# Feed-forward products of a decoder layer by one level of Strassen

## The chip, the cores and the metric

One core of a Trainium2 chip runs the whole program. Its engines are TensorE (PE in the profile, with its weight loads as PEld), VectorE (DVE), ScalarE (ACT), GpSimd (POOL) and SyncE (SP), which here only issues DMAs. The metric is device time in microseconds for one execution. The kernel before takes 2062.53 us, the median of 3 runs (2061.35 to 2063.6).

## The reference

One decoder layer is computed for 1024 prompt tokens and 32 sample tokens (8 sequences of 4), 1056 tokens in all, with model width 1024, in float32:

```python
x = x + 0.5 * _swiglu(_rms(x, g1), w1g, w1u, w1d)
z = _rms(x, gm) @ w_in                    # q, k, v, gate B, gate C, h
x = x + concat([att, gate_b * cv]) @ w_out
x = x + 0.5 * _swiglu(_rms(x, g2), w2g, w2u, w2d)
x = x + sigmoid(_rms(x, gp) @ wpg) * (pe @ wpp)

def _swiglu(h, w_gate, w_up, w_down):
    return (silu(h @ w_gate) * (h @ w_up)) @ w_down
```

The attention is over a sliding window of 128 with a sink for each head, and the convolution is causal with width 3. The feed-forward width is 2816, so the gate and up matrices are 1024 x 2816 and the down matrix is 2816 x 1024. There are two feed-forwards, and they hold 132 of the 166 weight units (a unit is 128 x 1024) that the kernel reads in its main stream.

## The kernel before

**Precision.** Each float32 product is made of three products of float32r parts. A weight or an activation w is split into hi (a rounded copy, made by ScalarE) and lo = w - hi (made by VectorE). `mm_group` (L266) then issues, for each block of 128 rows, hi x hi (L268), lo x hi (L269) and hi x lo (L270) into one PSUM bank.

**Layout.** Activations lie with the model dimension on the partitions: `x[c]` holds 8 blocks of 128 rows for the tokens of chunk c. There are three chunks of 384, 384 and 288 tokens.

**Weights.** All weight units form one list in order of use. `pump_dma` (L96) loads them on SP's queue into two raw buffers, `split_one` (L104) splits one unit on ScalarE (L110) and VectorE (L111), and up to five split units are held. `tick` (L130) counts groups of products. It splits a unit if there is room, and runs work that was put off with `after(d, fn)` until d groups later.

**Norm.** `prep` (L230) splits x times the gain, without the token's factor; `square` (L220) and `norm_r` (L243) compute `rb`, the factor 1/sqrt(mean square) for each token, by squares on ScalarE, adds on GpSimd (L228), a product with ones, and `rsqrt_chain` (L198) on VectorE. The factor multiplies what comes out of the products (L305, L309), so products can start before it is known. For the first feed-forward it comes from a token-major copy of x (L398 to L432).

**Feed-forward.** `ffn` (L282) goes through the 22 blocks of the feed-forward width in groups of 3, 3, 4, 4, 4 and 4. For each block, `gate` and `up` multiply a unit by the three chunks; `up` applies silu and leaves the hidden activation, split, in SBUF (`hh`, `hl`). After each group, `down` (L315) multiplies the group's blocks into the 8 output blocks and adds a quarter of that to `x` (L325). In the last group each output block is followed at once by `prep` and `square` for the next norm (L364 to L366).

**Between the feed-forwards** come the input projection, attention and convolution, worked in pieces between product groups, and the output projection. x waits in DRAM meanwhile (`xs_d`, L456), and `mix` takes its place in SBUF. At the end comes the gated embedding (L905 to L974).

**Order.** The order of each engine's instructions is fixed when the program is built, by the order in which the code names them and by when a model of the chip takes them to be ready. On the chip each engine takes its list in order. Five PSUM banks serve the large products and three the small ones.

## Time and profile before

| | |
|---|---|
| median of 3 runs | 2062.53 us |
| profiled execution: span from first to last instruction | 2060.6 us |
| what lies around the span, against the median | 1.9 us |
| TensorE busy | 2050.2 us (99%), 12683 matmuls |
| VectorE busy | 960.3 us (47%) |
| ScalarE busy | 501.5 us (24%) |
| GpSimd busy | 287.2 us (14%) |
| moved by DMA | 118.06 MB, 57 GB/s on average |

The span is one profiled execution; its time outside the span isn't shown, so it is compared with the median of the runs. A row of the grouped view names line, engine, operation, output and inputs, shapes and count, then the busy time of the group and the mean length of one instruction in ns, then the idle time of the engine before them and what ended it. Matmuls are pipelined: the length of one is its latency, and what a stream of them costs is the distance between their starts. A row of the view by windows gives the busy time of each engine in a stretch, the granted TensorE clock (1.00 is full speed), the DMA engines' share and GB/s.

### The profile page before, as it was taken

How to read it: one execution, taken by the hardware profiler on the slowest of the kernel's cores; microseconds unless marked ns; L12 is line 12 of the kernel's file. 1: busy time of each engine (PE TensorE's matmuls, PEld its weight loads, DVE VectorE, ACT ScalarE, POOL GpSimd, SP SyncE). 2: the span in 40 equal slices, each digit the busy share in tenths (PEclk: the TensorE clock that was granted, in tenths of full speed). 3: DMA queues.
4: the chain of work that ended last, by engine and by line, in shares of the span. 5: the costliest groups of instructions: out<-in, count | busy, mean ns of one | idle time of the engine just before them, and what ended most of it. 6: DMA issues, size and time to landing. Idle time of an engine off the chain costs nothing.

```text
span 2060.6 us, 29941 instructions
## 1 busy us (share of the span) xinstructions
PE 2050.2 (99%) x12683; PEld 2007.9 (97%) x12683; DVE 960.3 (47%) x1809; ACT 501.5 (24%) x917; POOL 287.2 (14%) x335
## 2 busy tenths in 40 slices
PE   9999999999999999999999999999999999999999
PEld 9999999999999999988888999999999999999999
DVE  6343433433334366466773764343333343344843
ACT  6121120211211243233442421212112022023410
POOL 3201010110100142022221220101101001012300
PEclk9999999999999999999999999999999999999999
DMA  7211110211111124111131211111111021111121
GB/s 263 76 54 42 52 52 11 83 41 51 43 32 62 42 102 136 35 31 32 31 93 36 70 52 41 49 38 50 40 52 52 21 72 42 31 62 52 59 71 39
DMA packets 37673, 118.06 MB, mean 57 GB/s; under 512 B 7697, under 2 KB 12185, under 8 KB 36644
## 3 DMA queue, kind: packets, MB, share of 16 engines
q1 hardware_dynamic: 35780, 112.05, 16.9%
q0 software_dynamic: 1472, 4.00, 0.7%
q8 instruction: 99, 1.62, 0.3%
q14 instruction: 34, 0.28, 0.0%
q10 hardware_dynamic: 288, 0.10, 0.0%
HBM read 106.26 MB, written 11.58 MB: 57 GB/s over the span
## 4 chain that ended last, share of the span: by engine, by line
PE 97%; DVE 2%; DMA 1%; ACT 0%; issue 0%; POOL 0%; ACTq 0%; DVEq 0%; POOLq 0%
PE ps L269 29%; PE ps L268 29%; PE ps L270 28%; PE ps L790 2%; PE ps L791 2%; PE ps L792 2%; PE ps L630 1%; PE ps L674 1%; PE ps L627 1%; PE ps L665 1%; PE ps L570 0%; DVE xnl L236 0%; DVE xr L325 0%; DVE wlo L111 0%; DVE nt L209 0%; DMA wraw<-in_wpg_dram 0%
## 5 line engine op out<-in xcount | busy, mean ns | idle before, releaser
L268 PE MATMUL ps<-xnh,whi 128*128 128x384 f32 (+1 forms) x2448 | 786.8, 322 | 1.2 <-ACT whi L110 1.2
L269 PE MATMUL ps<-xnh,wlo 128*128 128x384 f32 (+1 forms) x2448 | 786.7, 322 | 0.8 <-DVE wlo L111 0.8
L270 PE MATMUL ps<-xnl,whi 128*128 128x384 f32 (+1 forms) x2448 | 786.2, 321 | 0.0
L269 PEld LDWEIGHTS ps<-xnh,wlo 128*128 128x128 f32 x2448 | 460.0, 188 | 1.3 <-DVE wlo L111 1.1
L268 PEld LDWEIGHTS ps<-xnh,whi 128*128 128x128 f32 x2448 | 459.8, 188 | 1.5 <-ACT whi L110 1.4
L270 PEld LDWEIGHTS ps<-xnl,whi 128*128 128x128 f32 x2448 | 460.1, 188 | 0.2
L269 PE MATMUL ps<-hh,wlo 128*128 128x384 f32 (+1 forms) x1056 | 343.8, 326 | 0.0
L268 PE MATMUL ps<-hh,whi 128*128 128x384 f32 (+1 forms) x1056 | 341.5, 324 | 0.0
L270 PE MATMUL ps<-hl,whi 128*128 128x384 f32 (+1 forms) x1056 | 336.7, 320 | 0.0
L110 ACT CAST whi<-wraw 128x1024 fp32r<-128x1024 f32 x166 | 173.1, 1051 | 615.9 <-PE ps L270 523.0
L309 POOL TENSOR_TENSOR a<-a,rb 128x384 f32<-128x384 f32 x132 | 128.9, 977 | 1235.8 <-DVE a L308 1230.3
L111 DVE TENSOR_TENSOR wlo<-wraw,whi 128x1024 fp32r<-128x1024 f32 x166 | 213.5, 1290 | 106.8 <-ACT whi L110 106.6
L270 PEld LDWEIGHTS ps<-hl,whi 128*128 128x128 f32 x1056 | 198.1, 188 | 0.9 <-DVE hl L312 0.6
L269 PEld LDWEIGHTS ps<-hh,wlo 128*128 128x128 f32 x1056 | 198.1, 188 | 0.5
L268 PEld LDWEIGHTS ps<-hh,whi 128*128 128x128 f32 x1056 | 197.6, 187 | 0.3
L311 ACT CAST hh<-a 128x384 fp32r<-128x384 f32 x132 | 64.3, 487 | 366.9 <-POOL a L309 366.9
L305 DVE TENSOR_TENSOR a<-ps,rb 128x384 f32<-128x384 f32 x132 | 69.1, 524 | 178.3 <-PE ps L270 174.7
L312 DVE TENSOR_TENSOR hl<-a,hh 128x384 fp32r<-128x384 f32 x132 | 68.8, 521 | 152.0 <-ACT hh L311 152.0
L325 DVE SCALAR_TENSOR_TENSOR xr<-ps,xr 128x384 f32<-128x384 f32 (+1 forms) x144 | 75.2, 523 | 132.8 <-PE ps L270 132.6
L325 DVE SCALAR_TENSOR_TENSOR x<-ps,x 128x384 f32<-128x384 f32 (+1 forms) x144 | 75.1, 522 | 133.0 <-PE ps L270 132.9
L308 DVE TENSOR_TENSOR a<-a,ps 128x384 f32<-128x384 f32 x132 | 68.8, 521 | 126.3 <-PE ps L270 125.7
L306 ACT ACTIVATE th<-a 128x384 f32<-128x384 f32 x132 | 65.5, 496 | 225.8 <-DVE a L305 225.7
(190 smaller groups left out, 1828.6 us busy)
## 6 DMA issues: line engine op xcount, KB each, us to landing
wraw<-in_w1gu_dram SPq DMA_DIRECT2D x44, 512.0 KB
wraw<-in_w2gu_dram SPq DMA_DIRECT2D x44, 512.0 KB
wraw<-in_w1d_dram SPq DMA_DIRECT2D x22, 512.0 KB
wraw<-in_w2d_dram SPq DMA_DIRECT2D x22, 512.0 KB
wraw<-in_win_dram SPq DMA_DIRECT2D x18, 512.0 KB
xtok<-in_xtok_dram SPq DMA_DIRECT2D x8, 512.0 KB
wraw<-in_wout_dram SPq DMA_DIRECT2D x8, 512.0 KB
wraw<-in_wpg_dram SPq DMA_DIRECT2D x8, 512.0 KB
```

What stands on the lines that cost most here:

```text
L110: nc.scalar.copy(out=hi, in_=raw)
L111: nc.vector.tensor_tensor(out=lo, in0=raw, in1=hi.bitcast(F32), op=ALU.subtract)
L268: nc.tensor.matmul(ps[:, :W], lhsT=wh, rhs=xh, start=(k == 0), stop=False)
L269: nc.tensor.matmul(ps[:, :W], lhsT=wl, rhs=xh, start=False, stop=False)
L270: nc.tensor.matmul(ps[:, :W], lhsT=wh, rhs=xl, start=False, stop=(k == n - 1))
L305: nc.vector.tensor_tensor(out=a[:, :W], in0=psg[:, :W], in1=rb, op=ALU.mult)
L306: nc.scalar.activation(out=th[:, :W], in_=a[:, :W], func=AF.Tanh, scale=0.5)
L308: nc.vector.tensor_tensor(out=a[:, :W], in0=a[:, :W], in1=ps[:, :W], op=ALU.mult)
L309: nc.gpsimd.tensor_tensor(out=a[:, :W], in0=a[:, :W], in1=rb, op=ALU.mult)
L311: nc.scalar.copy(out=hh[j][:, sl], in_=a[:, :W])
L312: nc.vector.tensor_tensor(out=hl[j][:, sl], in0=a[:, :W], in1=hh[j][:, sl].bitcast(F32), op=ALU.subtract)
L325: nc.vector.scalar_tensor_tensor(out=x[c][:, m], in0=ps[:, :W], scalar=0.25, in1=x[c][:, m], op0=ALU.mult, op1=ALU.add)
```

## The change

Both feed-forwards are written anew; the projections, attention, convolution and embedding keep their products, with their memory pools opened and closed around them.

**Products.** The product of a 256-row pair of weight blocks with the activations is treated as a 2 x 2 matrix product of half-blocks, by a seven-product form of Strassen's method. The tokens are two halves (c) of 528, each of two quarters of 264; the model dimension has two halves of four 128-row blocks. For gate and up, "2 x 2" on the weight side is the two halves of the rows by gate and up; for down it is the two blocks of a pair by output blocks m and m + 4. Each of seven products is a sum of weight blocks times a sum of activation blocks, made of 264-column matmuls, three for each block of rows. Seven weight operands and seven activation operands are split into hi and lo. Products 1, 6, 7 and 4 accumulate in one PSUM bank with readings in between, 5 and 3 in a second, 2 in a third. `segment` interleaves one quad's products with the rest of the one before.

**Phases.** `gate_up` first makes the normalised activations of a token half (`normed`: squares, rb, then for each of 4 block pairs the sums on GpSimd and seven splits), then goes through the 22 blocks j with their two halves. The first two blocks run for the first half, then for the second (their weights are loaded twice), so that the second half's activations are made meanwhile. The hidden activations go to DRAM (`hd`). `down` reads them back in four groups of 2, 3, 3 and 3 pairs (`hidden`), makes their sums and splits, and adds the products to X.

**Norms.** `prep`, `square` and `norm_r` for the input projection and the embedding stand behind `down`, no longer within its last group.

```diff
-    def ffn(tag, name, g_next, name_next, s_next, skew):
...
+    def weights(pr, po, blocks, wd, shape):
+        r = []
+        for b in blocks:
+            t = pr.tile([P, wd], F32, name="wr", tag="wr", bufs=6)
+            nc.sync.dma_start(out=t.rearrange("p (k m) -> p k m", m=P), in_=b)
+            r.append(t)
+        s = [pr.tile([P, wd], F32, name="ws", tag="ws", bufs=4) for _ in range(4)]
+        add = nc.gpsimd.tensor_tensor
+        add(out=s[0], in0=r[2], in1=r[3], op=ALU.add)
+        add(out=s[1], in0=s[0], in1=r[0], op=ALU.add)
+        add(out=s[2], in0=r[0], in1=r[2], op=ALU.add)
+        add(out=s[3], in0=s[1], in1=r[1], op=ALU.add)
+        of = {1: r[0], 2: r[1], 3: s[3], 4: r[3], 5: s[0], 6: s[1], 7: s[2]}
+        for o in OPS:
+            hi = po.tile([P, wd], F32R, name=f"wh{o}", tag=f"wh{o}")
+            lo = po.tile([P, wd], F32R, name=f"wl{o}", tag=f"wl{o}")
+            split(hi, lo, of[o])
...
+        def product(self, o, ps, start):
+            wh, wl = self.w[o]
+            bh, bl = self.acts[o]
+            for k in range(self.n):
+                ks = slice(k * P, (k + 1) * P)
+                last = k == self.n - 1
+                nc.tensor.matmul(ps[:, :HH], lhsT=wh[:, ks], rhs=bh[:, k], start=(start and k == 0), stop=False, skip_group_check=True)
+                nc.tensor.matmul(ps[:, :HH], lhsT=wl[:, ks], rhs=bh[:, k], start=False, stop=False, skip_group_check=True)
+                nc.tensor.matmul(ps[:, :HH], lhsT=wh[:, ks], rhs=bl[:, k], start=False, stop=last, skip_group_check=True)
...
+    def segment(q, p):
+        for o, of in ((1, q), (5, q), (7, p), (2, q), (6, q), (3, p), (4, p)):
+            if of:
+                of.step(o)
...
+    class Down(Quad):
+        def add(self, x, h, ps, f):
+            s = slice(h * HH, (h + 1) * HH)
+            nc.vector.scalar_tensor_tensor(out=x[:, s], in0=ps[:, :HH], scalar=f, in1=x[:, s], op0=ALU.mult, op1=ALU.add)
...
+    def normed(pool, c, g):
...
+        for k in range(4):
+            y = [wtile(f"y{j}", shape=[P, 2, HH]) for j in range(2)]
+            for j in range(2):
+                kk = k + 4 * j
+                nc.vector.scalar_tensor_tensor(
+                    out=y[j].rearrange("p n t -> p (n t)"), in0=X[kk][c], scalar=vec[:, g + kk:g + kk + 1], in1=rb, op0=ALU.mult, op1=ALU.mult,
+                )
+            sums(acts, k, y[0][:, 0], y[0][:, 1], y[1][:, 0], y[1][:, 1], wtile("ta", shape=[P, 2, HH]), wtile("tb", shape=[P, 2, HH]))
+        return acts
+
+    def sums(acts, k, b11, b12, b21, b22, ta, tb):
+        nt3, nt1, nt2, nt4 = ta[:, 0], ta[:, 1], tb[:, 0], tb[:, 1]
+        tt = nc.gpsimd.tensor_tensor
+        tt(out=nt1, in0=b11, in1=b12, op=ALU.subtract)
+        tt(out=nt3, in0=b12, in1=b22, op=ALU.subtract)
+        tt(out=nt2, in0=nt3, in1=b11, op=ALU.subtract)
+        tt(out=nt4, in0=nt2, in1=b21, op=ALU.add)
...
+    def gate_up(gu, g, spill, mid=None):
...
+        plan = [(j, (0,)) for j in range(SKEW)] + [(j, (1,)) for j in range(SKEW)] + [(j, (0, 1)) for j in range(SKEW, FF)]
...
+    def down(dn, src):
...
+        def hidden(gi, c):
+            p0, n = DGROUPS[gi]
+            t = ph[0].tile([P, 2, 2, n, HH], F32, name="hr", tag="hr")
+            for i in range(2):
+                for h in range(2):
+                    o = c * HC + h * HH
+                    nc.sync.dma_start(out=t[:, i, h], in_=hd[2 * p0 + i:2 * (p0 + n) + i - 1:2, :, o:o + HH].rearrange("q p t -> p q t"))
+            a = {}
+            for o in OPS:
+                a[o] = tuple(pa[c][0].tile([P, n, HH], F32R, name=f"h{u}{o}", tag=f"h{u}{o}") for u in "hl")
...
+    gate_up(w1gu, G1, False, bias_table)
+    down(w1d, xin)
...
+    for c in range(3):
         for k in range(KT):
-            prep(c, k, G2)
+            prep(c, k, GP)
             square(c, k)
-        norm_r(c, "n2", 8)
...
+        norm_r(c, "np", 9, 4 if c < 2 else 2)
```

Each pool that `gate_up`, `down` and the middle part open takes SBUF that others have closed; a tile waits for the earlier tiles that lay there. Every tile of these pools has one buffer unless the code names more (6 raw weight tiles, 4 weight sums); each activation and weight operand has one.

551 lines of the change are left out of this document (322 added, 229 removed).

## The prediction

> **What bounds the kernel now.** I read the page's busy shares first, then the chain that ended last, then what TensorE waited for.
>
> ```profile
> PE 2050.2 (99%) x12683; PEld 2007.9 (97%) x12683; DVE 960.3 (47%) x1809; ACT 501.5 (24%) x917; POOL 287.2 (14%) x335
> PE 97%; DVE 2%; DMA 1%; ACT 0%; issue 0%; POOL 0%; ACTq 0%; DVEq 0%; POOLq 0%
> ```
>
> ```profile
> PE ps L268 <- ACT whi L110: 1.2, 1, 1.2
> ```
>
> TensorE is busy 99% of the span and is 97% of the chain; its longest wait is 1.2 us. So a matmul removed is time removed, as long as the other engines stay hidden, and only about 10 us in the whole span are idle to be won. VectorE has half the span free, GpSimd most of it.
>
> A matmul's price is its start-to-start distance, not its "mean ns" (that is latency, and matmuls overlap). A stretch of the timeline inside the first feed-forward gives it for both widths in use:
>
> ```profile
> 299.75 0.29 PE L268 MATMUL ps<-xnh,whi 128*128 128x288 f32 x1
> ...
> 302.15 0.34 PE L268 MATMUL ps<-xnh,whi 128*128 128x384 f32 x1
> ...
> 310.47 0.29 PE L268 MATMUL ps<-xnh,whi 128*128 128x288 f32 x1
> ```
>
> 18 matmuls of 288 columns start in 2.40 us (133.3 ns each), 48 of 384 in 8.32 us (173.3 ns). A line through both: 0.417 ns a column and 13.3 ns for each matmul whatever its width.
>
> **What is removed.** Each feed-forward has (44 gate and up units x 8 + 22 down units x 8) x 3 products x 3 chunks = 4752 matmuls; a triple of chunks takes 2 x 173.3 + 133.3 = 480 ns, so 1584 x 480 = 760 us. The change has 22 x 2 halves x 7 x 12 = 3696 and 11 x 4 x 2 x 7 x 3 = 1848, together 5544 matmuls of 264 columns: more matmuls, though an eighth fewer columns. At 264 columns the line gives 123.3 ns, 684 us. **Saved: 76.7 us each, 153 us for both**, not the 190 us that an eighth of 1520 would be. No row has 264 columns. If 264 columns cost what 288 do (133.3 ns), both save 42 us; if time were proportional to columns (122.2 ns), 166 us. I take the line, whose nearest point is 24 columns away.
>
> **What the other engines are given.** The rows that price it (mean ns is the number before the bar of idle time):
>
> ```profile
> L111 DVE TENSOR_TENSOR wlo<-wraw,whi 128x1024 fp32r<-128x1024 f32 x166 | 213.5, 1290 | 106.8 <-ACT whi L110 106.6
> L312 DVE TENSOR_TENSOR hl<-a,hh 128x384 fp32r<-128x384 f32 x88 | 49.1, 558 | 149.7 <-ACT hh L311 149.7
> L312 DVE TENSOR_TENSOR hl<-a,hh 128x288 fp32r<-128x288 f32 x44 | 19.6, 446 | 2.3 <-ACT hh L311 2.3
> L325 DVE SCALAR_TENSOR_TENSOR x<-ps,x 128x288 f32<-128x288 f32 x48 | 21.8, 455 | 31.5 <-PE ps L270 31.5
> L311 ACT CAST hh<-a 128x384 fp32r<-128x384 f32 x88 | 45.2, 514 | 346.2 <-POOL a L309 346.2
> L311 ACT CAST hh<-a 128x288 fp32r<-128x288 f32 x44 | 19.1, 434 | 20.7 <-POOL a L309 20.7
> L309 POOL TENSOR_TENSOR a<-a,rb 128x384 f32<-128x384 f32 x88 | 91.3, 1038 | 1137.4 <-DVE a L308 1131.9 <-ACT th L306 5.5
> L309 POOL TENSOR_TENSOR a<-a,rb 128x288 f32<-128x288 f32 x44 | 37.6, 854 | 98.3 <-DVE a L308 98.3
> ```
>
> Scaled to the new widths: DVE about 0.42 us at 264 columns, 0.56 at 384, 0.69 at 512, 0.98 at 792, and 0.43 for a 264-column add from PSUM; ACT 0.41 at 264, 0.62 at 512; POOL 0.80 at 264, 1.28 at 512, 1.82 at 792.
>
> In the middle of gate_up this hides. One j has 168 matmuls, 20.7 us; DVE does 7 x 0.69 + 14 x 0.42 = 10.7 us, ACT 7 x 0.62 + 8 x 0.41 = 7.6 us, POOL 4 x 1.28 + 2 x 0.80 = 6.7 us. I cost it at nothing; the cover is the 20.7 us, and even DVE and POOL in strict turns (17.4 us) fit.
>
> They may have to take turns:
>
> ```profile
> L111 DVE TENSOR_TENSOR wlo<-wraw,whi x166: 1208/1226/2071, 7.7 to 1984.6; 128x1024 fp32r<-128x1024 f32 x166
> L228 POOL TENSOR_TENSOR acc<-acc,sq x63: 803/1018/2253, 735.5 to 1941.8; 128x384 f32<-128x384 f32 x42, 128x288 f32<-128x288 f32 x21
> L325 DVE SCALAR_TENSOR_TENSOR x<-ps,x x144: 441/558/558, 84.5 to 780.9; 128x384 f32<-128x384 f32 x96, 128x288 f32<-128x288 f32 x48
> L236 DVE SCALAR_TENSOR_TENSOR xnl<-x,vec,xnh x48: 502/614/1369, 6.3 to 783.9; 128x384 fp32r<-128x384 f32 x32, 128x288 fp32r<-128x288 f32 x16
> ```
>
> (min/median/max ns.) The same DVE subtraction takes 1.23 us or 2.07 us, the same POOL add 1.02 or 2.25: the extra is about one operation of the other engine. The lines that lengthen have both operands in SBUF; the adds from PSUM (L325) never pass 0.56 us. The Trainium skill, "SBUF — State Buffer", section "Who interferes with whom", says that a VectorE instruction with two SBUF inputs and a GpSimd instruction that reads SBUF exclude each other for the whole instruction. By it every length below is the full sum of both engines; the maxima here agree with that direction.
>
> **The head of each feed-forward.** Today TensorE starts on raw x, since the token factor rb is applied behind the product. The new gate_up needs sums of normalised x, so squares, rb, sums and seven splits stand before the first product. For one half of the tokens: DVE 8 x 0.76 (the gain-times-rb step, L236's 614 stretched to 528 columns) + 28 x 0.42 = 17.9 us; POOL 16 x 0.80 = 12.8 us, in a chain of four each. Overlapped: 17.9 us; in turns: 30.7. I take 26, nearer the turns, because all of these DVE operations have both operands in SBUF, like the lines that lengthen. A weight set (7 splits, 4 adds) is 4.8 to 9.9 us, taken as 8.7. The second half has six more adds, 30 us in all.
>
> ```profile
> 0.74 3.51 DMA x<-in_xT_dram
> ...
> 7.73 0.44 PE L268 MATMUL ps<-xnh,whi 128*128 128x384 f32 x1 [1.15 <-ACT whi L110]
> ```
>
> ```profile
> 0.00:10.00 10.00, 6.94 (x31) 6.39 (x32) 3.69 (x9) 5.66 (x8) 1.22 (x7) 1.00 0.84 310
> 1920.00:1940.00 20.00, 20.00 (x138) 19.73 (x138) 18.75 (x42) 11.85 (x23) 9.16 (x10) 1.00 0.00 1
> 1940.00:1960.00 20.00, 17.19 (x92) 15.48 (x91) 18.50 (x42) 6.58 (x9) 2.59 (x2) 1.00 0.57 178
> ```
>
> (Windows: length, busy PE, PEld, DVE, ACT, POOL, then clock, DMA share, GB/s.) First feed-forward: half of x, 2.2 MB at 310 GB/s behind a first landing at 4.3 us, is there at about 10 us; the last square, add, statistics and rb end at about 16 us by my estimate. Then first half 26, its weights 8.7, second half 30, second weights 8.7: the third segment, the first on the second half, can start at 89 us. TensorE has then done 11 products of 12 matmuls, 16.3 us. Today it begins at 7.7 us and runs some 3 us slow: 89 - 16.3 - 7.7 - 3 = **+62 us** (overlapped +38, in turns +76). The skew of two j gives the second half a cover of those 16 us, against 30 and two weight sets. Second feed-forward: the first half of x is final four groups of 24 x 133.3 ns, 12.8 us, before the output projection ends, and some 6 us of squares, statistics and rb follow, so sums start 7 us before that end: -7 + 26 + 8.7 + 30 + 8.7 - 16.3 = **+50 us** (+26 to +64).
>
> **Entry to down.** The activations' trip through DRAM itself hides, since only the last j's store is fresh and the first group reads j 0 to 3. But the first weights wait for gate_up's buffers:
>
> ```profile
> 1944.45 4.48 DMA wraw<-in_wpg_dram
> ```
>
> A wait for a weight load like this one is 4.5 us, and a split behind it 1 us; the second half's sums then meet segments of only 5.2 us. In the first group (pairs, so 256-column weights) DVE has 28 x 0.41 + 56 x 0.43 + 14 x 0.71 = 45.5 us against TensorE's 41.4. Together 15 us, **+30** for both (10 to 50).
>
> **Group changes in down.** A group of three pairs is 62.2 us on TensorE; DVE has 28 x 0.56 + 56 x 0.43 + 14 x 0.98 = 53.5 us, POOL 16 x 1.04 + 8 x 1.82 = 31 us. Over the group it just fits, but the seven activation tiles and the one load buffer `hr` have no second copy: the second half's load is issued only when the first half's last direct split is done, some 0.8 us into the new group, and 1.6 MB at 310 GB/s plus two POOL sums and a split end at about 13.7 us, where product 6 is wanted at 12.2. With what queues on DVE I take 4 us a change, three a feed-forward: **+24** (10 to 72). SP issues in order, so weight loads behind that waiting load are late too; they have a spare set and half.
>
> **Norms behind down.** Today the last down group's products cover prep, square and the rsqrt chains, though DVE is then 18.75 of 20 us busy (row above). The new code starts them when down's memory is free, in the last three products.
>
> ```profile
> L207 DVE SCALAR_TENSOR_TENSOR nt<-rb 128x192 f32<-128x192 f32 x36 | 14.2, 428 | 0.0
> ```
>
> One chunk is 8 x 0.61 on DVE and up to 8 x 1.0 on POOL, 5 to 13 us, then up to 8 for its rsqrt chain (two halves x ten operations like this one), against 8.3 us of k and v products: **+15** before the input projection (4 to 25), **+12** before the embedding (2 to 25), where 2.8 us of TensorE idle exist already (last window). Reading x back before the output projection has five PSUM buffers of 4.2 us as cover: **+3** (0 to 10). Its stores lie beside k and v.
>
> **The clock.**
>
> ```profile
> 10.25:13.65 3.40, 3.40 (x13) 3.40 (x12) 3.00 (x6) 3.40 (x7) 0.00 (x0) 0.52 1.05 420
> ```
>
> After the waits at the start TensorE ran 3.4 us at half clock, 1.7 us lost. Some ten new stops could each bring one: 0 to 17 us, **+8** taken, as most stops end in work limited by DVE anyway. The Trainium skill, "TensorE: Matmul & The Clock Gate", section "Part 1", has the clock halve after an idle window of about 3.4 us; by that the sum would be 17 and the total 9 us higher.
>
> **Sum.** -153 + 62 + 50 + 30 + 24 + 15 + 12 + 3 + 8 = +51 us. The profiled span is 2060.6 us and the median 2062.5, so 1.9 us lie around the span: 2060.6 + 51 + 1.9 = **2114 us**.
>
> **Rivals.** (1) *The heads are short, and it is faster.* DVE and POOL overlap, and each head is as long as DVE alone: 38, 26, and the low ends elsewhere, 10 + 10 + 4 + 2: -153 + 90 = -63, about **2000 us**; with half the other terms 2025. For it: most L228 adds stay near 1.02 us. Against: the maxima above. It decides once a half takes under about 19 us. (2) *Strict turns everywhere, DVE the bound of down too.* Heads 76 and 64; each three-pair group is stretched to about 72 us by DVE waiting for half of POOL's 31, +10 a group and +14 in the first, 88 for both where I have 54: 51 + 28 + 34 = +113, **2175 us**. For it: the rows with maxima; against: DVE's 24 us of PSUM adds do not lengthen (L325) and can run beside POOL. The section of the Trainium skill named above states this rival's rule. (3) *A floor under the matmul.* 264 columns cost 133 ns: 111 us less saved, **2225 us**. For it: weight loads already fill PEld 97%; against: the distance falls with columns down to 288.
>
> **Chances.** Forecast 0.57 (its own range 2070 to 2155), rival 1 0.20, rival 2 0.18, rival 3 0.05. No change (within 0.2%, what a measurement here can tell) lies between rival 1 and the forecast: 0.04, taken from both. So faster 0.20, same 0.04, slower 0.76. The range 2015 to 2200 leaves out rival 3, the lower part of rival 1 and rival 2's tail.
>
> **What would show it.** Right: 264-column matmuls 123 ns apart; TensorE mostly idle from 10 to 90 us and again behind the output projection, released by DVE splits of activations and of weights; gaps of a few us at each new `hr`. Wrong: the third segment already under way at 65 us, or a steady gate_up in which TensorE waits, or down without gaps.

## The result: slower by 8.5%

The changed kernel takes 2237.99 us (median of 4 runs, 2235.64 to 2241.02), the kernel before 2063.02 us on the same chip (4 runs, 2061.35 to 2063.6). The ratio is 1.085, with a 95% interval of 1.0835 to 1.0865. The forecast was 2114 us with a range up to 2200: the sign was right, the size was not. Of the excess over before, 175 us, the sum had 51.

### The profile page after: what moved, and what is told of

It reads as the page before. It is cut to its first block, busy times and chain, and to the rows that moved or that the text cites. A ratio compares the mean times of both kernels' runs of the same rounds, so it can differ in the third digit from the quotient of the medians.

```text
span 2239.2 us, 37149 instructions
## 1 busy us (share of the span) xinstructions
PE 1977.0 (88%) x14387; PEld 1907.3 (85%) x14387; DVE 1521.7 (68%) x2723; ACT 782.0 (35%) x1636; POOL 822.9 (37%) x690
## 4 chain that ended last, share of the span: by engine, by line
PE 73%; DVE 17%; issue 4%; DMA 3%; ACT 2%; POOL 1%; SPq 0%; DVEq 0%; POOLq 0%; ACTq 0%
PE ps L360 17%; PE ps L362 17%; PE ps L361 17%; PE ps L295 4%; PE ps L296 4%; PE ps L297 4%; DVE wl L324 4%; DVE x L428 2%; PE ps L981 2%; PE ps L983 2%; PE ps L982 2%; DVE hl L324 2%; DVE bl L324 2%; DVE xnl L263 2%; DMA hr<-hd 1%
## 5 line engine op out<-in xcount | busy, mean ns | idle before, releaser
L360 PE MATMUL ps<-bh,wh 128*128 128x264 f32 x2464 | 708.8, 288 | 60.6 <-ACT wh L323 42.8
L362 PE MATMUL ps<-bl,wh 128*128 128x264 f32 x2464 | 704.5, 286 | 17.4 <-DVE bl L324 17.4
L361 PE MATMUL ps<-bh,wl 128*128 128x264 f32 x2464 | 706.7, 287 | 12.6 <-DVE wl L324 12.6
L360 PEld LDWEIGHTS ps<-bh,wh 128*128 128x128 f32 x2464 | 468.1, 190 | 65.5 <-ACT wh L323 44.0
L362 PEld LDWEIGHTS ps<-bl,wh 128*128 128x128 f32 x2464 | 469.4, 191 | 19.9 <-DVE bl L324 19.9
L361 PEld LDWEIGHTS ps<-bh,wl 128*128 128x128 f32 x2464 | 469.0, 190 | 14.7 <-DVE wl L324 14.5
L360 PE MATMUL ps<-hh,wh 128*128 128x264 f32 x1232 | 359.0, 297 | 51.6 <-DVE x L428 35.2
L361 PE MATMUL ps<-hh,wl 128*128 128x264 f32 x1232 | 358.5, 293 | 10.8 <-DVE wl L324 10.3
L362 PE MATMUL ps<-hl,wh 128*128 128x264 f32 x1232 | 353.7, 292 | 8.6 <-DVE hl L324 8.5
L360 PEld LDWEIGHTS ps<-hh,wh 128*128 128x128 f32 x1232 | 239.0, 196 | 62.9 <-DVE x L428 34.4
L428 DVE SCALAR_TENSOR_TENSOR x<-ps,x 128x264 f32<-128x264 f32 x448 | 182.4, 424 | 66.4 <-PE ps L362 65.4
L295 PE MATMUL ps<-xnh,whi 128*128 128x384 f32 (+1 forms) x336 | 114.5, 344 | 47.3 <-ACT whi L125 31.6
```

The costliest lines, as they stand in the source:

```text
L295: nc.tensor.matmul(ps[:, :W], lhsT=wh, rhs=xh, start=(k == 0), stop=False)
L360: nc.tensor.matmul(ps[:, :HH], lhsT=wh[:, ks], rhs=bh[:, k], start=(start and k == 0), stop=False, skip_group_check=True)
L361: nc.tensor.matmul(ps[:, :HH], lhsT=wl[:, ks], rhs=bh[:, k], start=False, stop=False, skip_group_check=True)
L362: nc.tensor.matmul(ps[:, :HH], lhsT=wh[:, ks], rhs=bl[:, k], start=False, stop=last, skip_group_check=True)
L428: nc.vector.scalar_tensor_tensor(out=x[:, s], in0=ps[:, :HH], scalar=f, in1=x[:, s], op0=ALU.mult, op1=ALU.add)
```

## The profile after

The page of the changed kernel: span, busy shares, TensorE in 40 slices of 56 us, its granted clock, the chain. The profiled execution is the slowest of the four, 3 us above their median.

```profile
span 2239.2 us, 37149 instructions
...
PE 1977.0 (88%) x14387; PEld 1907.3 (85%) x14387; DVE 1521.7 (68%) x2723; ACT 782.0 (35%) x1636; POOL 822.9 (37%) x690
...
PE   4599999997898977999998747999999978999589
...
PEclk6699999999999987999999868999999989999799
...
PE 73%; DVE 17%; issue 4%; DMA 3%; ACT 2%; POOL 1%; SPq 0%; DVEq 0%; POOLq 0%; ACTq 0%
```

TensorE's busy time fell by only 73 us and its idle time rose from 10 to 262 us. VectorE, which had 2% of the chain, now has 17%. The slices show where: at the two heads of the feed-forwards (slices 0, 1 and 23, 24), at the entry to down and in it (9 to 12, 32 and 33) and behind it (14, 15 and 37).

The timeline gives the stretches. First the kernel before, where the first matmul of each next stage marks a bound; then the changed kernel, where the number in brackets is TensorE's idle time ahead of the matmul.

```profile
776.73 0.34 PE L268 MATMUL ps<-xnh,whi 128*128 128x384 f32 x1
...
1171.85 0.34 PE L268 MATMUL ps<-xnh,whi 128*128 128x384 f32 x1
...
1936.15 0.34 PE L268 MATMUL ps<-xnh,whi 128*128 128x384 f32 x1
```

```profile
42.91 0.59 PE L360 MATMUL ps<-bh,wh 128*128 128x264 f32 x1 [21.62 <-ACT wh L323]
...
539.67 0.28 PE L362 MATMUL ps<-bl,wh 128*128 128x264 f32 x1
546.25 0.59 PE L360 MATMUL ps<-hh,wh 128*128 128x264 f32 x1 [6.30 <-ACT wh L323]
...
821.96 0.28 PE L362 MATMUL ps<-hl,wh 128*128 128x264 f32 x1
835.10 0.69 PE L295 MATMUL ps<-xnh,whi 128*128 128x384 f32 x1 [12.85 <-ACT whi L125]
...
1270.05 2.28 PE L472 MATMUL ps<-ones,acc 128*128 128x1 f32 x24
...
1302.70 0.59 PE L360 MATMUL ps<-bh,wh 128*128 128x264 f32 x1 [20.68 <-ACT wh L323]
...
1795.97 0.28 PE L362 MATMUL ps<-bl,wh 128*128 128x264 f32 x1
1802.52 0.59 PE L360 MATMUL ps<-hh,wh 128*128 128x264 f32 x1 [6.27 <-ACT wh L323]
...
2076.18 0.28 PE L362 MATMUL ps<-hl,wh 128*128 128x264 f32 x1
```

| stretch, us | before | after | difference |
|---|---|---|---|
| first feed-forward, to the last product of down | 776.7 | 822.1 | +45.4 |
| middle: input projection to output projection | 395.1 | 448.0 | +52.9 |
| second feed-forward | 764.3 | 806.2 | +41.9 |
| tail: embedding | 124.5 | 162.9 | +38.4 |
| span | 2060.6 | 2239.2 | +178.6 |

Half of the loss lies outside the feed-forwards, where no product was changed. Windows of the changed kernel (length, busy PE, PEld, DVE, ACT, POOL, then clock, DMA share, GB/s) show the stages from within:

```profile
42.90:140.00 97.10, 70.04 (x469) 64.93 (x470) 85.86 (x130) 43.31 (x98) 57.02 (x45) 0.77 0.28 89
140.00:540.00 400.00, 399.95 (x3267) 398.95 (x3266) 239.56 (x407) 138.05 (x288) 139.55 (x122) 1.00 0.25 78
546.20:622.00 75.80, 60.62 (x404) 55.82 (x405) 71.64 (x115) 31.06 (x58) 48.94 (x39) 0.89 0.42 133
...
684.00:760.00 76.00, 67.20 (x531) 65.03 (x530) 69.15 (x104) 29.32 (x49) 40.16 (x28) 1.00 0.29 88
...
822.00:840.00 18.00, 2.50 (x8) 1.46 (x6) 17.71 (x34) 15.02 (x37) 13.03 (x19) 0.58 0.44 139
```

In the middle of gate and up TensorE is never idle. In the head, in down and behind down VectorE is busy 88%, 95%, 91% and 98% of the time and TensorE waits. What it waits for, by the view of waits (total, times, longest):

```profile
PE ps L360 <- ACT wh L323: 55.8, 7, 21.6
PE ps L360 <- DVE x L428: 35.2, 32, 2.8
PE ps L295 <- ACT whi L125: 31.6, 4, 17.9
PE ps L361 <- DVE wl L324: 22.8, 14, 2.5
PE ps L362 <- DVE bl L324: 17.4, 8, 3.0
```

Four of the seven waits for `wh` in L360 are the first products of gate and up and of down in the timeline above. The 32 waits for `x` are in down: a PSUM bank is held until VectorE has added it to x, and that add stands in VectorE's list behind splits. The groups of VectorE and GpSimd by form say why the list is slow (the second number after the count, before the bar, is the mean ns of one):

```profile
L324 DVE TENSOR_TENSOR wl<-ws,wh 128x512 fp32r<-128x512 f32 x192 | 149.3, 780 | 35.2 <-ACT wh L323 34.6
L324 DVE TENSOR_TENSOR wl<-wr,wh 128x512 fp32r<-128x512 f32 x144 | 145.1, 1007 | 17.3 <-ACT wh L323 13.5 <-DMA wr<-in_w2gu_dram 0.2
...
L324 DVE TENSOR_TENSOR hl<-hr,hh 128x792 fp32r<-128x792 f32 x36 | 49.5, 1375 | 7.3 <-ACT hh L323 7.3
L324 DVE TENSOR_TENSOR bl<-y,bh 128x264 fp32r<-128x264 f32 x48 | 32.8, 720 | 0.0
...
L428 DVE SCALAR_TENSOR_TENSOR x<-ps,x 128x264 f32<-128x264 f32 x448 | 182.4, 424 | 66.4 <-PE ps L362 65.4
```

```profile
L501 POOL TENSOR_TENSOR hta<-hr 128x792 f32<-128x792 f32 x12 | 27.1, 2258 | 0.0
L502 POOL TENSOR_TENSOR htb<-hta,hr 128x792 f32<-128x792 f32 x12 | 26.9, 2242 | 0.5
```

The splits, whose operands are both in SBUF, are well above the lengths that the prediction scaled from before (0.69 us at 512 columns, 0.98 at 792, 0.42 at 264); GpSimd's sums at 792 columns are above its 1.82. The adds from PSUM (L428) have 424 ns, near the 0.43 us of the prediction.

## Experiments: are the turns of VectorE and GpSimd the cause?

All times below stand against runs of the kernel before on the same chip; the difference to the changed kernel is taken to its 2238.0 us. Intervals are 95%. The kernel before had medians of 2062.7 to 2063.9 us beside them. Each edit was run twice, and two executions of one kernel lie up to 5 us apart, so a difference below that tells little; stretches of a trace come from one execution.

**No sums.** GpSimd's additions are left out of the computation, and the plain blocks serve as operands of the seven products.

```diff
-        add(out=s[0], in0=r[2], in1=r[3], op=ALU.add)
...
-        of = {1: r[0], 2: r[1], 3: s[3], 4: r[3], 5: s[0], 6: s[1], 7: s[2]}
+        of = {1: r[0], 2: r[1], 3: r[1], 4: r[3], 5: r[2], 6: r[2], 7: r[0]}
```

> The changed kernel without the sums that GpSimd makes for the seven products: each operand is a plain block in place of a sum (the four weight adds of each set and the four activation subtractions of each step are left out, so the output is another one). TensorE, ScalarE and VectorE issue the same instructions. Theory A, VectorE and GpSimd take turns and this lengthens the heads and down: VectorE's 264-column splits fall from 0.97 to 0.42 us, a token half in a head from 23 to some 16 us, the stalls in down mostly go: 100 to 130 us less, 2110 to 2140 us. Theory B, VectorE's own splits and adds set the pace and GpSimd works in their shadow: at most 25 us less, 2213 us or more.

Measured: 2102.35 us, ratio 1.0192 (1.0162 to 1.0222): 136 us less, more than theory A had; it is still 39 us above the kernel before. Gate and up start at 23.4 us and take 484.6 (42.9 and 496.9 with sums), down takes 234.7 instead of 275.8. The middle stays at 445.0 us and the tail at 162.7: their loss has another cause.

**The same sums, read by nobody.** The run above takes away two things at once: GpSimd's use of SBUF, and the wait for a sum ahead of a split. Here GpSimd adds as in the change, but into tiles that nothing reads.

```diff
-        of = {1: r[0], 2: r[1], 3: s[3], 4: r[3], 5: s[0], 6: s[1], 7: s[2]}
+        of = {1: r[0], 2: r[1], 3: r[1], 4: r[3], 5: r[2], 6: r[2], 7: r[0]}
```

> The products take the plain blocks as operands, as in the run without sums (2102 us), but GpSimd still does every weight and activation addition of the change, into tiles that nothing reads; the seven sums so have no part in the output. Theory A1 (turns): what cost 136 us there was GpSimd being busy at all, because its additions and VectorE's splits with both operands in SBUF take turns. Then most of it comes back: 2180 to 2240 us, the 512-wide weight splits still 0.8 to 1.0 us in the mean, the 792-wide activation splits 1.2 us or more. Theory A2 (waiting for the sums): it was the splits waiting behind chains of four additions. Then nothing reads the sums, nobody waits, and it stays at 2100 to 2125 us, the 512-wide split nearer 0.7 us.

Measured: 2251.84 us, ratio 1.0909 (1.0878 to 1.0941). All of the 136 us came back and 14 more, above the range of theory A1; why it is more was not isolated. The splits by form, without the additions and with additions that nobody waits for:

```profile
L324 DVE TENSOR_TENSOR wl<-wr,wh 128x512 fp32r<-128x512 f32 x336 | 246.9, 738 | 84.5 <-ACT wh L323 80.2
...
L324 DVE TENSOR_TENSOR hl<-hr,hh 128x792 fp32r<-128x792 f32 x60 | 58.6, 979 | 8.8 <-ACT hh L323 8.8
L324 DVE TENSOR_TENSOR bl<-y,bh 128x264 fp32r<-128x264 f32 x80 | 30.7, 433 | 0.0
```

```profile
L324 DVE TENSOR_TENSOR wl<-wr,wh 128x512 fp32r<-128x512 f32 x336 | 333.4, 1005 | 36.2 <-ACT wh L323 34.4
...
L324 DVE TENSOR_TENSOR hl<-hr,hh 128x792 fp32r<-128x792 f32 x60 | 84.0, 1403 | 12.1 <-ACT hh L323 12.1
...
L324 DVE TENSOR_TENSOR bl<-y,bh 128x264 fp32r<-128x264 f32 x80 | 56.3, 749 | 0.0
```

The same 336 subtractions on the same operands take 738 ns or 1005, those of 792 columns 979 or 1403, those of 264 columns 433 or 749. No sum passes from GpSimd to a split in the second run, so it is GpSimd being at work that lengthens them. Sorted by whether a GpSimd instruction runs at the same time, 147 of the 336 stand alone and have 688 ns in the mean, the other 189 have 1251; the adds from PSUM have 424 to 426 ns either way. Raw tiles that GpSimd holds longer are no rival: the casts of 512 columns waited 25.1 us for their DMA without the additions, 21.9 with them. This is the rule of the Trainium skill, "SBUF — State Buffer", section "Who interferes with whom": a VectorE instruction with two SBUF inputs and a GpSimd instruction that reads SBUF exclude each other. The pair of runs agrees; 149 us lie between them.

**The sums on VectorE.** If two engines take turns, one can do both works at the cost of its own. The heads' sums and the weight sums of gate and up go to VectorE; those of down stay on GpSimd.

```diff
-        add = nc.gpsimd.tensor_tensor
+        add = (nc.vector if wd == 512 else nc.gpsimd).tensor_tensor
...
-        tt = nc.gpsimd.tensor_tensor
+        tt = (nc.gpsimd if k is None else nc.vector).tensor_tensor
```

> The sums of both heads and of the gate and up weights are made on VectorE instead of GpSimd; down is unchanged. Theory A: a half in a head costs VectorE 8 x 0.68 + 44 x 0.34 = 20.4 us without being blocked, against 23 us now, and weight sets no longer block it: 10 to 25 us less, 2213 to 2228 us. Theory B: VectorE has a third more to do in the heads, 15 to 30 us more, 2253 to 2268 us.

Measured: 2212.5 us, ratio 1.0726 (1.0695 to 1.0757), 25.5 us less. The 512-wide split is back at 701 ns and the 264-wide one at 436, gate and up start at 38.8 us and take 487.6; down, where nothing was changed, keeps 274.1. In the heads the second engine made the work slower, not faster.

## Experiments: where do the seven products pay?

**Down by eight products.** The four plain blocks, no sums, four splits for a set of operands instead of seven; gate and up as in the change.

```diff
-                q = Down(w, acts[c] if not (m == 0 and c == 1) else None, DGROUPS[gi][1], m, c)
...
-                segment(q, prev)
+                for s in range(2):
+                    for h in range(2):
+                        ps = plain(w, acts[c], DGROUPS[gi][1], s, h)
+                        xs = X[m + 4 * s][c][:, h * HH:(h + 1) * HH]
+                        nc.vector.scalar_tensor_tensor(out=xs, in0=ps[:, :HH], scalar=0.25, in1=xs, op0=ALU.mult, op1=ALU.add)
```

> The down products by eight half-blocks instead of seven, with no sums and four splits instead of seven; phases, groups, buffers and the way through DRAM stay. TensorE's own work in a down phase goes from 228 to 260 us. Theory A/B (the seven-product operands overload VectorE and GpSimd in down): down becomes TensorE-bound, 265 to 272 us with its entry against 282 now, 20 to 34 us less in all, 2204 to 2218 us. Rival: the stalls in down come from the phase itself (the single load buffer, the entry's wait for buffers), they stay, and the kernel is 50 to 65 us slower, 2290 to 2303 us.

Measured: 2173.99 us, ratio 1.0539 (1.0509 to 1.057): 64 us less with 528 more matmuls. Two windows of this run, the second of them the one that the changed kernel's row above covers:

```profile
622.00:684.00 62.00, 62.00 (x512) 62.00 (x511) 27.70 (x52) 14.67 (x24) 0.00 (x0) 1.00 0.32 98
684.00:760.00 76.00, 76.00 (x627) 76.00 (x626) 30.94 (x59) 15.72 (x26) 0.94 (x1) 1.00 0.28 87
```

TensorE is busy throughout, VectorE 41% in the second window, where it was 91% with seven products. Down takes 259.5 us for 2112 matmuls, against 275.8 for 1848. The middle shrank from 448.0 to 431.9 us and the tail from 162.9 to 144.8, which I had not expected: the expectation of at most 34 us less held for down itself (16 us each), and the other half came from behind it.

**All by eight products, phases kept.** Down as above, gate and up too.

```diff
-            sums(acts, k, y[0][:, 0], y[0][:, 1], y[1][:, 0], y[1][:, 1], wtile("ta", shape=[P, 2, HH]), wtile("tb", shape=[P, 2, HH]))
+            for i in range(2):
+                for h in range(2):
+                    split(acts[i, h][0][:, k], acts[i, h][1][:, k], y[i][:, h])
```

> All feed-forward products by eight half-blocks, no seven-product operands anywhere; the phases, the normalisation before the product, the way through DRAM and the norms behind down stay. TensorE's own work is that of 264-column matmuls, 22 x 2 x 8 x 12 + 11 x 4 x 2 x 8 x 6 = 6336 a feed-forward, 781 us, 41 us more for both than before the change. If the seven-product operands cause most of the loss (theory A): 2063 + 41 + heads of some 30 and 20 + norms behind down of some 80 and entries of 12: about 2245 us, as slow as the change although it does an eighth more products. If the phases cause the loss whatever the products: 195 us of products more than the change, less 64 for down: 2300 us or more.

Measured: 2209.01 us, ratio 1.0707 (1.0676 to 1.0738).

```profile
100.00:557.00 457.00, 457.00 (x3759) 457.00 (x3757) 117.96 (x232) 76.86 (x156) 0.00 (x0) 1.00 0.21 66
557.00:563.20 6.20, 0.37 (x3) 0.16 (x2) 3.04 (x6) 1.86 (x4) 0.00 (x0) 0.94 0.71 221
563.20:823.60 260.40, 260.40 (x2112) 260.02 (x2112) 109.44 (x220) 61.61 (x118) 13.26 (x14) 0.99 0.32 100
```

That is below both expectations: I had put the norms behind down at 80 us, and by the stretches they cost 55. The run splits the change in two. The new layout, with no product saved, costs 146 us over before: 2 x 14 for 264-column matmuls in place of 384 and 288 (6336 x 122.2 ns = 774 against 760 us), about 33 in each feed-forward for its head and its entry to down, 35 in the middle, 20 in the tail. The seven products then take away 1584 matmuls, 194 us, and give back 223; 136 of these go when the sums are left out, and the rest isn't divided further. With this run and the one before: seven products in gate and up win 35 us net, in down they lose 64.

## Experiments: heads, clock and the norms behind down

**A faster clock in the heads.** 24 matmuls whose result nobody reads stand behind each of the first three activation steps.

```diff
+            if k < 3:
+                fill = psb(sm)
+                for _ in range(24):
+                    nc.tensor.matmul(fill[:, :HH], lhsT=acts[1][0][:, k, :P], rhs=acts[1][0][:, k], start=True, stop=True)
```

> 24 matmuls whose result is not used behind each of the first three activation steps of each token half in both heads, so that TensorE is not idle there. Theory C, the half clock behind idle stretches costs time of its own: the clock stays up in the heads and up to 7 us a head are saved, 5 to 15 us less, 2223 to 2233 us. Rival: in the heads TensorE waits for operands anyway and the clock is worth nothing: 2235 to 2245 us, with the granted clock higher all the same.

Measured: 2237.57 us, ratio 1.0848 (1.0812 to 1.0883), no gain. The same two windows of the changed kernel and of this run:

```profile
22.90:60.00 37.10, 14.17 (x86) 13.06 (x87) 36.29 (x51) 21.99 (x52) 28.47 (x23) 0.63 0.13 42
60.00:100.00 40.00, 16.75 (x83) 13.27 (x81) 35.31 (x53) 14.43 (x36) 26.06 (x24) 0.59 0.26 81
```

```profile
22.90:60.00 37.10, 27.21 (x147) 25.15 (x148) 35.96 (x49) 21.60 (x51) 29.03 (x23) 0.76 0.15 43
60.00:100.00 40.00, 27.37 (x167) 25.10 (x165) 35.31 (x55) 14.46 (x36) 25.77 (x24) 0.77 0.28 81
```

The clock rises from 0.6 to 0.77, VectorE is busy 97 to 98% and 88% in both, and gate and up end at 538.0 instead of 539.8 us. In the heads the low clock costs nothing, since VectorE's results set the pace.

**No second making of the first weights.** Each j does both token halves from the start (`SKEW = 2` becomes 0).

> The first two j's of gate and up are no longer done first for one half of the tokens and then, with their weights loaded, added and split a second time, for the other: each j does both halves at once, as the later ones do. Theory S (supply): in the head VectorE and GpSimd set the pace, so two weight sets fewer (each 28 us of the trace's head for about three sets, 8.7 us by my sum) are worth more than the products done early: 15 us less a feed-forward, 2200 to 2220 us in all. Theory K (cover): the two early segments, 16 us of products, are what covers the second half's sums. Without them TensorE is idle for 16 us more each time and saves 8.7 to 17 of weight sets: 2230 to 2255 us.

Measured: 2229.19 us, ratio 1.08 (1.0768 to 1.0831), 8.8 us less: between the two theories. By the stretches gate and up and their heads are 5.3 us shorter and down, which the edit doesn't touch, 4.3; so how much of the gain is the skew's isn't shown. The early segments cover no more than the extra weight sets cost.

**Statistics of the second feed-forward ahead of the last projection groups.**

```diff
...
+            if m0 == 4 and c == 1:
+                rb0 = token_rb(0)
...
```

> Squares, statistics and rb of the first token half of the second feed-forward are named before the last four groups of the output projection, as the prediction took for granted. If the late statistics are what made this head 20 us longer than predicted: the first product of that head starts 10 to 20 us earlier, 2218 to 2228 us. Rival: VectorE's splits and weight sets set the pace there and the third segment comes no earlier: under 5 us, 2233 us or more.

Measured: 2235.21 us, ratio 1.0834 (1.0803 to 1.0866), 3 us less, within what such a pair of runs can tell. The first product comes 21.3 us behind the projection instead of 32.7, and in the profiled execution the second feed-forward is 10.3 us shorter (795.9 against 806.2); the middle, where the statistics now stand, is 4.2 us longer. The two medians show 3 us of that.

**Order behind down.** At 822 us ScalarE has 32 pieces of `prep` ahead of the split of the first weight unit, by the timeline of the changed kernel:

```profile
821.05 13.07 ACT L262 ACTIVATE xnh<-x,vec 128x384 fp32r<-128x384 f32 x32
834.02 1.97 ACT L125 CAST whi<-wraw 128x1024 fp32r<-128x1024 f32 x2
```

So the first matmul comes at 835.10. Three runs take that stretch apart, each with the same edit before the embedding. The first names the weight units behind the first chunk's `prep`; the second also puts all squares of a chunk ahead of its `prep`; the third, from the first, makes the additions of squares on VectorE.

```diff
             prep(c, k, GM)
             square(c, k)
+        if c == 0:
+            wget(UNIT["win"])
+            wget(UNIT["win"] + 1)
...
```

> Behind each down, the first weight units (two before the input projection, one before the embedding) are named right behind the first chunk's prep, no longer behind all three chunks' preps. Theory D, the order on ScalarE's queue (32 preps ahead of the first weight split) makes the 13 us gap before the first product: that product starts 5 to 8 us earlier in both places and 8 to 14 us are saved, 2224 to 2230 us. Rival E: the token factor rb is what comes last there, the products only run ahead into five PSUM banks and wait for it later: 0 to 4 us saved, 2234 to 2238 us.

Measured: 2228.6 us, ratio 1.0802 (1.0771 to 1.0833), 9.4 us less.

```diff
-            prep(c, k, GM)
             square(c, k)
+        for k in range(KT):
+            prep(c, k, GM)
...
```

> As the run before, and each chunk's eight squares stand before its preps, so that the statistics come first. Theory E, rb comes last: another 10 to 25 us saved, 2205 to 2225 us. Theory D: no more than the run before.

Measured: 2231.35 us, ratio 1.0815 (1.0783 to 1.0848): no better than the first. The further gain fell: GpSimd's additions still ended near 855 us (855.8, and 855.5 in the first).

```diff
-            nc.gpsimd.tensor_tensor(out=accs[c][:, :W], in0=accs[c][:, :W], in1=sq[:, :W], op=ALU.add)
+            nc.vector.tensor_tensor(out=accs[c][:, :W], in0=accs[c][:, :W], in1=sq[:, :W], op=ALU.add)
...
```

> As the run with the first weight units named behind the first chunk's preparation (2228.6 us), and the additions of squares before the input projection and before the embedding are made by VectorE instead of GpSimd. Theory P: GpSimd's 21 additions of about 1.1 us in one row, each waiting its turn against VectorE, end some 15 us after the squares and hold the rsqrt chain that TensorE waits for (idle 860 to 875 us); on VectorE they take 0.56 us each behind the splits: 10 to 20 us less, 2208 to 2220 us. Theory V: VectorE is the bound there (it is busy 15 of 18 us), its 21 additions, 12 us a place, go on the same path: 2225 to 2240 us.

Measured: 2215.83 us, ratio 1.0735 (1.0704 to 1.0766): 12.8 us less than the first, so GpSimd's row of additions did hold the chain: in the first run its last 15 take 17.7 us in one row and end at 855.5, on VectorE the last ends at 842.6. The middle is now 437.6 us and the tail 153.0.

**Four edits that helped, together.** Down by eight products, the sums of gate and up and the additions of squares behind down on VectorE, first weight units named early.

> All edits that were thought to help at once: down by eight half-blocks without sums, gate and up by seven products with all weight and activation sums on VectorE, first weight units behind the first chunk's preparation, additions of squares on VectorE. If the gains add (64 + 25 + 9 + some 10 from 2238) it takes about 2130 us, still slower than before by 3%. If they overlap, since all of them shorten waits for VectorE, 2145 to 2165 us. For it to beat the kernel before, the phases themselves would have to cost nothing, which the run with plain products throughout (2209 us) speaks against.

Measured: 2142.55 us, ratio 1.038 (1.035 to 1.041). The four single gains add to 112 us; together they give 95. It still loses 79 us to before; of the 80 between the two spans 17 and 13 are in the feed-forwards, 34 in the middle (428.7 us) and 17 in the tail (141.0).

**Squares inside the last group of down**, on top of that run. Their accumulator gets a buffer of its own, and the work pool has six buffers instead of seven:

```diff
+                if gi == len(DGROUPS) - 1 and c == 1:
+                    for cc in range(3):
+                        square(cc, m)
+                        square(cc, m + 4)
...
```

> As the combined run (2142.6 us), and the squares and their additions for the norm behind down are no longer made behind its last products: each row of x is squared in the last group of down as soon as both halves of it are final, so that only the last two of eight rows are left behind the end. Theory N (the norm starts late): the middle of the combined run lasts 428.7 us against 394.9 before and its tail 141.0 against 124.4, 15.0 and 19.7 us of it TensorE idle, because squares, statistics and reciprocal roots all begin at the end of down. With 18 of the 24 squares gone from there both come 8 to 12 us sooner: 2115 to 2128 us. Rival T (the preparation is the bound): VectorE's 24 splits of x, 13 us by their length alone, stand behind the end in either case, and the squares' additions are moved onto a VectorE that is busy 10 of 14 us in the last group: 2135 to 2145 us.

Measured: 2144.02 us, ratio 1.039 (1.036 to 1.042), no gain in all. The stretches say more: the middle is 5.6 us shorter than in the combined run (423.1) and the tail 2.7 (138.1), where theory N had 8 to 12 us for each, and the second feed-forward is 8.8 us longer (786.4 against 777.6), for which no cause was isolated. From the end of down to where the first keys can be written:

```profile
794.50:820.80 26.30, 21.38 (x126) 20.62 (x124) 25.59 (x80) 14.50 (x34) 1.51 (x4) 0.99 0.34 107
```

VectorE is busy 25.59 of 26.30 us with all but the last additions of squares gone from there: 32 splits of x and the reciprocal-root chains of two chunks fill most of it. In the kernel before the same work lay under the products of the last down group.

**And no second making of weights**, on top of that:

> As the run with early squares, and each j of gate and up does both halves at once from the first, with no weight set made twice. With every sum on VectorE a weight set costs it 7 x 0.69 + 4 x 0.69, about 7.6 us, more than in the change, so theory S2 has 15 us of VectorE's work saved per head against 16 us of products done early: 5 us sooner to 5 us later than the run with early squares, as the same edit gave -9 in the change's own kernel. If it were over 10 us sooner, the repeated weight sets would be a cost of the head that the prediction left out; if over 10 us later, the two early segments would be the cover that it counted on.

Measured: 2134.18 us, ratio 1.0342 (1.0312 to 1.0372): 9.8 us less, more than the 5 us either way of the expectation. It is not plainly the weight sets' gain: against the combined run, which makes them twice, the feed-forwards are as long (1571.8 us for both, 1571.5 there), and the 8 us between the two runs lie behind down (middle 422.7, tail 138.5), where the early squares are. This is the fastest form that I found; it doesn't beat the kernel before.

## Why the prediction was right or wrong

| step of the sum, us | predicted | measured in the trace |
|---|---|---|
| removed products | -153 | -166 |
| heads of both feed-forwards | +112 | +142 |
| entry to down and group changes | +54 | +111 |
| norms behind down, before and after | +30 | +91 |
| clock | +8 | within the rows above, some 18 of the 91 |
| sum | +51 | +179 (rounded rows: 178) |

The measured rows are the stretches less their products at 122.2 ns (3696 for gate and up, 1848 for down): the first head is 42.9 + (496.9 - 451.6) = 88.2, less the 16.4 that before spends beside its 760.3 us; entry and down are 6.4 + (275.8 - 225.8) = 56.4; the second feed-forward alike (74.5 - 4.0, and 54.4).

**Removed products: right, at the other end.** 3267 matmuls in 400 us are 122.4 ns, 2457 in a 300 us window inside it 122.1. The line through two widths gave 123.3; time proportional to columns, which I had as an end of the range, gives 122.2 and fits. The third rival (a floor of 133 ns) is out.

**Heads: the wait was right, what stands before it was under-counted by 30.** TensorE stood idle in both heads as described, and what it waited for were splits. A half of the activations was priced well: 26 us in the sum, 23.4 in the trace for the first half (21.8 to 45.2; its last four splits stand among those of the weights) and 25.8 for the second (78.7 to 104.5). The first and last rows of VectorE for the two halves, and its first row for the second feed-forward:

```profile
21.80 2.38 DVE L491 SCALAR_TENSOR_TENSOR y<-x,vec,rb 128x528 f32<-128x528 f32 x2 [3.98 <-POOL ws L337]
...
42.95 2.21 DVE L324 TENSOR_TENSOR bl<-y,bh 128x264 fp32r<-128x264 f32 x3
...
78.73 1.45 DVE L491 SCALAR_TENSOR_TENSOR y<-x,vec,rb 128x528 f32<-128x528 f32 x2 [3.97 <-ACT rb L483]
...
104.08 0.42 DVE L321 SCALAR_TENSOR_TENSOR bl<-tb,bh 128x264 fp32r<-128x264 f32 x1
...
1282.55 1.45 DVE L491 SCALAR_TENSOR_TENSOR y<-x,vec,rb 128x528 f32<-128x528 f32 x2 [4.00 <-ACT rb L483]
```

What failed is the time around the halves. In the first head VectorE begins at 21.8 us, where the sum had 16, and 33.6 us lie between the halves, where it had 12.7 (one weight set, 8.7, and six more adds, 4): a second weight set, part of a third, and the second half's statistics stand there in VectorE's list as well. So TensorE runs without waits from 101 us on, where the sum had 89. In the second head the sum let the activations start 7 us ahead of the projection's end; they start 12.4 us behind it (at 1282.6, the projection ends at 1270.2), and that is 19 of the 20 us that this head is over. The turns have a share in the lengths: with the sums on VectorE the first product comes 4 us sooner and gate and up take 9 us less. The skew, whose cover is 16 us in the sum, is at best paid for by its second weight sets: without both the kernel is no slower.

**Entry and groups of down: the step that failed in kind.** I counted 53.5 us of VectorE and 31 of GpSimd a group, held that "over the group it just fits" in 62.2, and costed only the change of groups. But the turns last through the group. By the starts of their first matmuls, groups of three pairs take 69.6 to 72.0 us, where 504 products at 122.2 ns are 61.6, and the first group 62, where its 336 are 41. Without the sums they take 61.9 to 64.8 and 46 us, with sums that nobody reads 72.2 to 74.8 and 60. So GpSimd's additions beside VectorE's work set the pace of the whole group, and a PSUM bank waits for its add behind lengthened splits (32 waits, 35.2 us). The waits that the sum did price, for the new activations of a group, are 11.1 us in the trace (2.6 for `hh`, 8.5 for `hl`) against 24. The second rival, strict turns with VectorE the bound of down too, had this mechanism and priced it at 88 us; it measured 111. Its working, 53.5 us and half of 31, gives 69 us a group and not the 72 that it states; the groups came to 71. What it had too low is the first group, 21 us over its products and not 14, and it had no separate term for the 6.3 us of idle time ahead of it. I argued against it that the adds from PSUM do not lengthen. They don't (424 ns), but they stand in VectorE's list behind instructions that do.

**Norms behind down: the step most under-sized, 91 for 30.** I saw what was moved, and took only the time by which one chunk's work exceeds the products of k and v. Three things were left out: the first weight unit's split queues behind 32 pieces of `prep` on ScalarE (9.4 us for both places), GpSimd's row of additions ends 13 us later than VectorE's does (12.8 us more), and the splits of three chunks and the chains of two fill VectorE for 26 us behind down (in the run with early squares). The rest of it is only bounded by the runs: plain products in down take 16 + 18 us out of these stretches, without any edit there. I take that to be the work that seven products leave to VectorE at the end of down, but no run isolates it. Not all of the 91 is the norms': 9.9 us of TensorE's idle time in the middle come after 900 us, 6.7 of them waits for attention's `S` and 3.2 a wait for `x` in the output projection, where the kernel before has 0.3 us in the whole middle. Reading x back beside attention was put at 3 us; whether it makes the last of these waits isn't shown.

**Clock: wrong in form, harmless in the heads, too small behind down.** I charged 1.7 us for each stop. The clock stayed low for whole stretches, but where it did so in the heads it cost nothing (the filler run). Behind down the same matmuls keep TensorE busy 406.1 us in the middle, 394.8 before, and 123.7 in the tail, 117.4 before: 18 us. Of that busy time 24.8 and 11.7 us fall into stretches at half clock, and half of their sum is 18 us too. Whether a full clock would only have made the waits longer there, no run shows.

**The first rival** (short heads, faster) needed a half under 19 us. It took 23 to 26 in the trace.

**The chances.** 0.76 on slower was right; the range ended at 2200 because the rivals were priced one at a time. Every term that was wrong but the products erred to the same side. I read one common reason in most of them, VectorE's list, which is longer and slower than I took it for; the place of the second head's statistics, ScalarE's order and the clock are others.

## What to carry to other kernels

Before trading TensorE's work for additions and splits, compare what VectorE and GpSimd get to do with TensorE's time stage by stage, and not over the span, and count their SBUF instructions against each other. By the lengths of the prediction a block of gate and up has 17.4 us for the two in turns under 20.7 us of matmuls, and there the seven products paid; a group of three pairs in down has 53.5 and 31 us under 62, took 71, and there they lost. A loop that is split into phases loses the cover that its tail gave to the next stage: with plain products 55 of the 146 us that the new layout costs lie behind down. Where the engines that prepare operands are the bound, a better clock brought nothing and an earlier start of one link 3 to 9 us; leaving operands away (64 us) and taking the second engine out of the way (25.5 us) brought more.

## What the runs showed of the hardware

The turns of VectorE and GpSimd reach further than the extremes of the trace before let me think: with GpSimd adding, the mean of 80 splits of 264 columns rose from 433 to 749 ns, though GpSimd passed nothing to them. VectorE's adds from PSUM are not lengthened (424 ns), but they come late behind instructions that are: TensorE waits 35.2 us for them in down, and 0.8 us in the run without the sums.

The clock can stay at half through a stretch of short waits. In this window of the changed kernel the waits were for `bh` and `bl`, the longest 3.0 us (by the view of waits 2.8 for `bh`, 3.0 for `bl`), and TensorE was busy a quarter of the time at a granted clock of 0.50:

```profile
80.00:100.00 20.00, 4.99 (x11) 2.86 (x11) 20.00 (x28) 9.78 (x26) 13.89 (x16) 0.50 0.37 108
```

The Trainium skill, "TensorE: Matmul & The Clock Gate", section "Part 1", has the clock come back only after a window of some 3.4 us of sustained work. This stretch agrees with that side of the rule: from 101.25 us the matmuls follow each other 0.22 us apart without a wait, and 0.12 us apart only from 104.7, 3.5 us later; my term had used only the other, one loss for each long stop.
